# Channel mixers: where an older tile's GELU and product stand in the next tile's weight splitting

## The chip, the core and the metric

The kernel runs as one program on one core of a Trainium2 chip. The metric is the device time of one execution in microseconds (us). Three timed runs of the kernel before the change gave 1258.20, 1258.93 and 1259.92 us; the median is 1258.93 us.

Engines are named as the profile names them: PE multiplies matrices (PEld loads its stationary operand), DVE (VectorE) works element by element on whole tiles, ACT (ScalarE) applies functions and casts, POOL (GpSimd) here only issues DMAs that add into their destination, SP (SyncE) issues the plain loads.

## The reference, cut to what matters

A trunk of two layers works on 512 tokens of width 1024 in float32. Each layer ends in a convolutional GLU, the channel mixer, and the change lies in that alone:

```
def conv_glu(h, w_in, conv_w, conv_b, w_out):
    seq = h.shape[1]
    gate, val = jnp.split(h @ w_in, 2, axis=-1)
    gp = jnp.pad(gate, ((0, 0), (CONV_W - 1, 0), (0, 0)))
    conv = conv_b + sum(conv_w[j] * gp[:, j:j + seq] for j in range(CONV_W))
    return (jax.nn.gelu(conv, approximate=False) * val) @ w_out
```

`h @ w_in` has 2 x 2816 columns: 22 tiles of 128 gate columns and 128 value columns. For each tile the gate gets a causal convolution over three tokens with a bias, then GELU, and is multiplied by the value.

## The kernel before, in words

`ffn` (L435) is the channel mixer of one layer; it runs twice, once in each layer. The stage of interest is its middle: 21 of the 22 column tiles are worked off by `Seven.frame`, one call (a "frame") for each tile, and the last tile by `ending` (L648). In the trace the frames of layer 0 lie at about 390 to 587 us and those of layer 1 at about 935 to 1131 us.

**The arithmetic of a frame.** The tile's products are made by seven half-size matrix products in place of eight, so the weights first have to be added up: beside the loaded blocks G1, G2, V1, V2 of `raw` there are the sums S3, S1 (`sums`, L513, L515 in the profile), S2 (`sum2`, L520) and S4 (`sum4`, L524), all made by DVE. To keep float32 accuracy each operand is split in two parts: a rounded one, `whi`, that ACT makes with a cast (`high`, L528), and the remainder, `wlo`, which is raw minus `whi` (`lower`, L533, by DVE). One product (`prod`, L448) is 12 matmuls of 128x128 by 256 columns: 8 with `whi` (L452) and 4 with `wlo` (L454); `high_part` (L460) and `low_part` (L465) are the same in two pieces. A frame has seven of them, 84 matmuls.

**The next tile's first pair.** While frame j runs its last products, the weights of tile j+1 (`nxt`) are prepared. Its first pair is G1 beside S2: `nxt.high(G1)` casts both (128x1024) once `sum2` has made S2, and then comes the remainder, in one of two ways. For the tiles in `APART` (2, 4, ... 18) G1's remainder is made by ACT and an adding DMA (`rest1`, L505 and L506) and DVE subtracts only the S2 half (`both`, L510, 128x512). For the other tiles DVE subtracts the whole pair (`lower`, L533, 128x1024). So odd frames (3, 5, ... 17) have the short subtraction and even ones and frame 19 the long one. PE needs `whi` and `wlo` of that pair in the first product of frame j+1. Of the value pair, G2 beside V2, the remainder `wlv` is always made by ACT (`rest`, L499) and an adding DMA (L500).

**The tail of older tiles.** What is left of a tile after its products runs through the two frames behind it. In frame j the tile before, `prev`, gets `end1` (L539), `endr` (L542), `end2` (L555: the convolution's last tap and bias, by ACT), `endt` (L545: the first tap, scaled by ACT into a spare tile), `end3` (L559: the middle tap, by DVE) and `endd` (L552: an adding DMA issued by POOL that adds `endt`'s tile into the sum `c`). The tile before that one, `prev2`, gets `end4` (L562: GELU of `c`, by ACT, which has to wait for the DMA of `endd` of one frame earlier) and `end5` (L566: `c` times the value `v`, by DVE).

**What sets the order.** Nearly all of these instructions go through `keep` (L471), which holds them in the order in which the code is written, engine by engine. Each engine works its queue off in order, so an instruction that waits holds everything behind it on that engine. Small tiles (`tmp`) come from a pool of six buffers.

**The end of the stage.** `ending` is a generator that frames 19 and 20 step through. It loads the 22nd tile's gate weights (`raw_w`, L226, into a buffer that the next-to-last `wlv` leaves), casts them by ACT (L207, behind `end2` of tile 19, L555), subtracts by DVE (L215), and finishes tiles 18 to 21. The dense products of tile 21 are on L257, L258 and L261. Behind it comes `out_by_seven`, the output projection.

Of the kernel before, what the change touches and what calls it, by code (L numbers as in the profile page):

```python
# [90 lines left out]
def halved(t):  # L91
    return t.rearrange("p (a b) -> p a b", a=2)


def plain_order(ps):
    return ps.rearrange("p (b a) -> p a b", a=2)
# [37 lines left out]
def trunk_kernel(ctx, tc, A, out):  # L134
# [52 lines left out]
    def ps_f():  # L187
        return banks["F"].tile([P, S], F32, name="psf", tag="psf")
# [8 lines left out]
    def tmp(dt=F32, shape=(P, S)):  # L197
        return banks["tmp"].tile(list(shape), dt, name="tmp", tag="tmp")
# [67 lines left out]
    def run(g):  # L266
        for y in g:
            assert not callable(y) or y()
# [166 lines left out]
    def ffn(l, hp, U, T, new_x, xT, after=None, tokens=None):  # L435
# [10 lines left out]
        def prod(ps, w, x, late=False):  # L446
            (wh, wl), o, *ol = w
            ol = ol[0] if ol else o  # L448
            for ks in ((0, 1, 2), (3,)) if late else (range(4),):
                for k in ks:  # L450
                    for n in range(2):
                        PE.matmul(ps, wh[:, o + k * P:o + k * P + P], x[k][n], start=k == n == 0, stop=False)  # L452
                for k in ks:
                    PE.matmul(ps, wl[:, ol + k * P:ol + k * P + P], x[k][0], start=False, stop=k == 3)  # L454

        def high_part(ps, w, x):
            (wh, _), o = w
            for k in range(4):
                for n in range(2):
                    PE.matmul(ps, wh[:, o + k * P:o + k * P + P], x[k][n], start=k == n == 0, stop=False)  # L460

        def low_part(ps, w, x):
            (_, wl), o = w
            for k in range(4):
                PE.matmul(ps, wl[:, o + k * P:o + k * P + P], x[k][0], start=False, stop=k == 3)  # L465
# [3 lines left out]
        def keep(ins):  # L469
            return tc.keep_in_program_order(ins) if pinned[0] else ins  # L470

        h1, h2 = slice(0, 256), slice(256, 512)
        G1, S2, G2, V2, S3, S1, V1 = range(7)
        S4 = V1

        class Seven:
# [28 lines left out]
                keep(SC.activation(self.low1[:, :S], self.raw[:, G1], AF.Copy, scale=-1.0))  # L505
                GP.dma_start(self.low1[:, :S], A["ffn_in"][l, self.j, 0][:, 0:S], accum_op=ALU.add)  # L506

            def both(self):
                hi = self.high(G1)
                keep(V.tensor_tensor(self.low1[:, S:2 * S], self.raw[:, S2], hi[:, S:2 * S], op=ALU.subtract))  # L510
                self.gs = hi, self.low1

# [55 lines left out]
            def frame(self, prev2, prev, nxt, norm=None, ending=None):  # L568
                first = prev is None
                if first:  # L570
                    nxt.load()
                f1, f2, f3, self.f4 = (ps_f() for _ in range(4))
                g = self.g = tmp()
                prod(f1[:, h1], (self.gs, 0), XU(0, 0))
                if first:
                    hv = self.hv
                    turns["whi"] = (turns["whi"] + 1) % 3
                    self.h31 = self.high(S3)
                    turns["whi"] = (turns["whi"] + 1) % 3
                else:  # L580
                    hv = self.high(G2)
                keep(SC.copy(halved(g[:, h1]), plain_order(f1[:, h1])))
                if nxt and nxt.apart:
                    nxt.rest1()
                if first:
                    prod(self.f4[:, h1], ((hv, self.lows[0]), 0), XU(1, 0), True)
                if norm and not first:
                    run(norm)
                w31 = self.lower(S3, self.h31)
                if prev:  # L590
                    prev.end1()
                    prev.endr()
                prod(f2[:, h1], (self.gs, S), XT(T2), first)
                w4 = self.lower(S4, self.high(S4, S), S)
                if self.j + 2 < NFF - 1:
                    made[self.j + 2].load()
                if nxt and prev:
                    prev.end2()
                    prev.endt()
                elif prev:  # L600
                    next(ending)
                    next(ending)
                keep(V.tensor_tensor(halved(g[:, h2]), halved(g[:, h1]), plain_order(f2[:, h1]), op=ALU.subtract))
                if nxt:
                    nxt.sums()
                    nxt.sum2()
                    nxt.rest()
                if nxt and prev:
                    prev.end3()
                    prev.endd()  # L610
                if nxt and prev2:
                    prev2.end4()
                    prev2.end5()
                c = self.c = tmp()
                prod(f1[:, h2], (w31, 0), XT(T3))
                keep(V.tensor_tensor(halved(c[:, h1]), plain_order(f1[:, h2]), halved(g[:, h2]), op=ALU.subtract))
                if first:
                    next(norm)
                prod(f3[:, h2], (w31, S), XT(T1))
                if nxt:  # L620
                    if nxt.apart:
                        nxt.both()
                    else:
                        nxt.gs = nxt.lower(G1, nxt.high(G1))
                    nxt.sum4()
                else:
                    next(ending)
                if first:
                    next(norm)
                v = self.v = tmp()  # L630
                if first:
                    prod(f3[:, h1], ((hv, self.lows[1]), S, 0), XT(T4))
                else:
                    both = ((f3[:, h1], ((hv, self.low), S), XT(T4)), (self.f4[:, h1], ((hv, self.low), 0), XU(1, 0)))
                    for p in both:
                        high_part(*p)
                    low_part(*both[0])
                keep(V.tensor_tensor(v[:].rearrange("p (h a b) -> p h a b", h=2, a=2), halved(c[:, h1]).unsqueeze(1).to_broadcast([P, 2, 2, P]),
                                     f3[:].rearrange("p (h b a) -> p h a b", h=2, a=2), op=ALU.add))
                keep(V.tensor_tensor(halved(g[:, h2]), halved(g[:, h2]), plain_order(f3[:, h2]), op=ALU.subtract))  # L640
                if nxt:
                    nxt.h31 = nxt.high(S3)
                else:
                    next(ending)
                if not first:
                    low_part(*both[1])
                prod(self.f4[:, h2], (w4, 0), XU(1, 1))
# [1427 lines left out]
```

## Time and profile before

| what | us |
|---|---|
| median of the three runs | 1258.93 |
| lowest and highest run | 1258.20 and 1259.92 |
| the profiled execution's own time | 1260.42 |
| its span, first to last instruction | 1258.7 |
| PE busy (share of the span) | 1220.2 (97%) |
| DVE busy | 1028.8 (82%) |
| ACT busy | 841.8 (67%) |
| POOL busy | 150.9 (12%) |

The profiled execution took 1.7 us more than its span, and 1.5 us more than the median of the runs. PE's granted clock is at 90% or more in all 40 slices of the span, 0.997 on the mean. Busy shares are means over stages with different limits: in the frames (412 to 575 us) DVE is busy for 157.1 of 162.4 us, far above its 82%. Matmuls overlap in the records, so PE counts as busy even where its next matmul starts late; whether PE waits is read from the starts of its matmuls and from what ended the idle time, not from its share.

### The profile page before, as it was taken

The page shows a single profiled execution, that of the slowest core. Times are in us where ns is not written, and L with a number is a line of the kernel's source. Part 1 is how long each engine was busy: PE and PEld are TensorE (multiplying, and loading weights), DVE is VectorE, ACT ScalarE, POOL GpSimd, SP SyncE. Part 2 cuts the span into 40 slices and gives each one's busy share as a digit, 9 for nine tenths or more (in the row PEclk, how much of TensorE's full clock was granted, in tenths as well). Part 3 has the DMA queues.
Part 4 walks back from the last instruction along what each step waited for, and adds up shares of the span by engine and source line. Part 5 has one row for each costly group of instructions (what it writes and reads, how often), then busy time and mean ns, then how long its engine had stood idle before and what let it go on. Part 6 is the DMA issues. An engine that isn't in the chain of part 4 may idle for free.

```text
span 1258.7 us, 26447 instructions
## 1 busy us (share of the span) xinstructions
PE 1220.2 (97%) x10420; PEld 1074.6 (85%) x10420; DVE 1028.8 (82%) x1958; ACT 841.8 (67%) x1396; POOL 150.9 (12%) x180
## 2 busy tenths in 40 slices
PE   8999999999999999999999999999999999999997
PEld 6787777777788999999888878777789999998886
DVE  7976677766679999999876976658789999999785
ACT  6566668766566777776654676767767776765662
POOL 1000000000001222221220000000002322211200
PEclk9999999999999999999999999999999999999999
DMA  6355444453064989995994332234418998977961
GB/s 209 113 166 117 93 112 91 84 115 102 7 201 96 210 205 208 211 206 135 306 225 134 103 108 68 84 109 134 132 48 195 217 206 204 203 177 250 247 174 67
DMA packets 95293, 191.10 MB, mean 152 GB/s; under 512 B 22080, under 2 KB 30400, under 8 KB 95168
## 3 DMA queue, kind: packets, MB, share of 16 engines
q1 hardware_dynamic: 68592, 129.14, 32.3%
q0 software_dynamic: 26576, 60.26, 27.4%
q8 instruction: 82, 1.34, 0.4%
q14 instruction: 43, 0.35, 0.1%
HBM read 173.15 MB, written 6.29 MB: 143 GB/s over the span
## 4 chain that ended last, share of the span: by engine, by line
PE 61%; DVE 15%; ACT 9%; DMA 8%; issue 5%; POOL 1%; SPq 0%; DVEq 0%; ACTq 0%; POOLq 0%
PE psf L452 10%; PE psf L735 7%; PE psf L454 5%; PE psf L460 4%; PE psd L261 4%; PE psf L740 3%; PE psd L735 3%; PE psd L257 3%; PE psd L258 3%; DVE wlo L215 2%; DMA tmp<-r1h 2%; PE psf L465 2%; PE psd L740 2%; PE pss L1855 1%; ACT whi L207 1%
## 5 line engine op out<-in xcount | busy, mean ns | idle before, releaser
L528 ACT CAST whi<-raw 128x1024 fp32r<-128x1024 f32 (+1 forms) x168 | 150.7, 937 | 22.8 <-PE psf L452 17.4
L207 ACT CAST whi<-wraw 128x1024 fp32r<-128x1024 f32 x84 | 87.3, 1046 | 71.0 <-PE psd L258 33.8
L452 PE MATMUL psf<-th,whi 128*128 128x256 f32 x512 | 122.5, 278 | 2.0 <-ACT whi L528 2.0
L452 PE MATMUL psf<-tl,whi 128*128 128x256 f32 x512 | 122.3, 277 | 0.0
L533 DVE TENSOR_TENSOR wlo<-raw,whi 128x1024 fp32r<-128x1024 f32 (+1 forms) x108 | 109.2, 1013 | 2.0 <-ACT whi L528 1.9
L257 PE MATMUL psd<-r1h,whi 128*128 128x512 f32 x264 | 104.1, 395 | 0.0
L258 PE MATMUL psd<-r1l,whi 128*128 128x512 f32 x264 | 101.7, 386 | 0.0
L452 PEld LDWEIGHTS psf<-th,whi 128*128 128x128 f32 x512 | 98.9, 194 | 2.5 <-ACT whi L528 2.4
L452 PEld LDWEIGHTS psf<-tl,whi 128*128 128x128 f32 x512 | 99.2, 194 | 0.0
L215 DVE TENSOR_TENSOR wlo<-wraw,whi 128x1024 fp32r<-128x1024 f32 x67 | 81.8, 1221 | 20.5 <-ACT whi L207 20.5
L725 ACT CAST whi<-raw 128x1024 fp32r<-128x1024 f32 (+1 forms) x52 | 49.4, 950 | 53.1 <-PE psf L735 27.3
L726 DVE TENSOR_TENSOR wlo<-raw,whi 128x1024 fp32r<-128x1024 f32 (+1 forms) x52 | 56.7, 1101 | 30.5 <-ACT whi L725 27.8
L500 POOL DMA_DIRECT2D wlv<-in_ffn_in_dram x40 | 48.2, 1204 | 250.9 <-ACT wlv L499 193.1
L454 PE MATMUL psf<-th,wlo 128*128 128x256 f32 x504 | 77.7, 277 | 0.0
L261 PE MATMUL psd<-r1h,wlo 128*128 128x512 f32 x264 | 70.4, 389 | 0.9 <-DVE wlo L215 0.9
L555 ACT ACTIVATE tmp<-tmp,vec 128x512 f32<-128x512 f32 x44 | 35.9, 816 | 51.0 <-DVE tmp L542 51.0
L454 PEld LDWEIGHTS psf<-th,wlo 128*128 128x128 f32 x504 | 67.0, 193 | 0.1
L257 PEld LDWEIGHTS psd<-r1h,whi 128*128 128x128 f32 x264 | 49.9, 189 | 9.0 <-issue 2.1
L258 PEld LDWEIGHTS psd<-r1l,whi 128*128 128x128 f32 x264 | 50.0, 189 | 6.4 <-issue 0.7
L261 PEld LDWEIGHTS psd<-r1h,wlo 128*128 128x128 f32 x264 | 47.9, 189 | 8.0 <-DVE wlo L215 1.3
L515 DVE TENSOR_TENSOR raw<-raw 128x1024 f32<-128x1024 f32 x42 | 51.3, 1220 | 0.0
L257 PE MATMUL psd<-r2h,whi 128*128 128x512 f32 x128 | 50.3, 394 | 0.5 <-ACT r2h L1705 0.3
(622 smaller groups left out, 3739.5 us busy)
## 6 DMA issues: line engine op xcount, KB each, us to landing
raw<-in_ffn_in_dram SPq DMA_DIRECT2D x42, 512.0 KB, 5.2
raw<-in_ffn_in_dram SPq DMA_DIRECT2D x84, 256.0 KB, 5.9
wlv<-in_ffn_in_dram POOLq DMA_DIRECT2D x40, 512.0 KB, 7.8
raw<-in_ffn_out_dram SPq DMA_DIRECT2D x30, 512.0 KB, 5.8
raw<-in_ffn_out_dram POOLq DMA_DIRECT2D x24, 512.0 KB, 9.5
wraw<-in_wA_dram SPq DMA_DIRECT2D x20, 512.0 KB, 4.1
wraw<-in_w_out_dram SPq DMA_DIRECT2D x16, 512.0 KB, 4.0
wraw<-in_ffn_outp_dram SPq DMA_DIRECT2D x16, 512.0 KB, 4.7
```

The lines of the kernel that those rows point to most:

```text
L207: high = lambda: pin(SC.copy(hi[:, :n], raw))
L215: pin(V.tensor_tensor(lo[:, :n], raw, hi[:, :n], op=ALU.subtract))
L257: PE.matmul(ps, wh[:, j * P:(j + 1) * P], ah, start=start and n == 0, stop=False)
L258: dense_at[0] = PE.matmul(ps, wh[:, j * P:(j + 1) * P], al, start=False, stop=False)
L261: dense_at[0] = PE.matmul(ps, wl[:, j * P:(j + 1) * P], moving(act(k))[0], start=False, stop=stop and n == len(ks) - 1)
L452: PE.matmul(ps, wh[:, o + k * P:o + k * P + P], x[k][n], start=k == n == 0, stop=False)
L454: PE.matmul(ps, wl[:, ol + k * P:ol + k * P + P], x[k][0], start=False, stop=k == 3)
L528: keep(SC.copy(hi[:, :n], self.pair(what) if n > S else self.raw[:, what]))
L533: keep(V.tensor_tensor(lo[:, :n], self.pair(what) if n > S else self.raw[:, what], hi[:, :n], op=ALU.subtract))
L726: V.tensor_tensor(lo, s_, hi, op=ALU.subtract)
L735: PE.matmul(ps[:], a[:, k0 + i, ts], woven(hi[:, i * S:i * S + S]), start=bool(first) and (first is True or t in first) and a is act[0] an ...
L740: PE.matmul(ps[:], act[0][:, k0 + i, ts], woven(lo[:, i * S:i * S + S]), start=False, stop=bool(last) and t in last and i == n - 1)
```

## The change

In `frame`, the two calls `prev2.end4()` and `prev2.end5()` move. Before, they stood in front of `c = self.c = tmp()`, that is behind `end3` and `endd` of `prev`. Now the cast of the next tile's first pair, `nxt.high(G1)`, is taken out of `both` and of the call of `lower`; behind it stands `end4`, then the subtraction (`both` or `lower`), then `end5`, then `sum4`. Since `prev2` is there from frame 2 on and `nxt` up to frame 19, 18 frames of each layer are changed. Nothing is added or taken away.

```
@@ both @@
-            def both(self):
-                hi = self.high(G1)
+            def both(self, hi):
                 keep(V.tensor_tensor(self.low1[:, S:2 * S], self.raw[:, S2], hi[:, S:2 * S], op=ALU.subtract))
                 self.gs = hi, self.low1
@@ frame @@
                 if nxt and prev:
                     prev.end3()
                     prev.endd()
-                if nxt and prev2:
-                    prev2.end4()
-                    prev2.end5()
                 c = self.c = tmp()
                 prod(f1[:, h2], (w31, 0), XT(T3))
                 keep(V.tensor_tensor(halved(c[:, h1]), plain_order(f1[:, h2]), halved(g[:, h2]), op=ALU.subtract))
...
                 prod(f3[:, h2], (w31, S), XT(T1))
                 if nxt:
+                    hi = nxt.high(G1)
+                    if prev2:
+                        prev2.end4()
                     if nxt.apart:
-                        nxt.both()
+                        nxt.both(hi)
                     else:
-                        nxt.gs = nxt.lower(G1, nxt.high(G1))
+                        nxt.gs = nxt.lower(G1, hi)
+                    if prev2:
+                        prev2.end5()
                     nxt.sum4()
```

Lines behind `both` have a number lower by one in the changed file (L528 is L527, L562 is L561, L566 is L565), and L616, the subtraction that makes `c`, is L612.

ACT's queue in a frame, before: `rest`, the GELU, the three casts of G1, S3 and G2, the copy of `g`, and the cast of S4.

```order
L499 ACTIVATE wlv<-raw 128x1024
L562 ACTIVATE tmp<-tmp 128x512
L528 CAST whi<-raw 128x1024 x3
L582 COPY tmp<-psf 128x256
L528 CAST whi<-raw 128x512
```

The same stretch of ACT's queue now:

```order
L499 ACTIVATE wlv<-raw 128x1024
L527 CAST whi<-raw 128x1024
L561 ACTIVATE tmp<-tmp 128x512
L527 CAST whi<-raw 128x1024 x2
L581 COPY tmp<-psf 128x256
L527 CAST whi<-raw 128x512
```

The GELU has moved behind the first of the three casts.

DVE's queue in an odd frame (short subtraction), before, from `sums` to `sum4`: L559 is `end3`, L566 `end5`, L616 makes `c`, L510 is the subtraction of the next tile's first pair.

```order
L515 TENSOR_TENSOR raw<-raw 128x1024
L520 TENSOR_TENSOR raw<-raw 128x512
L559 SCALAR_TENSOR_TENSOR tmp<-tmp,vec 128x511
L566 TENSOR_TENSOR sp<-tmp 128x512
L616 TENSOR_TENSOR tmp<-psf,tmp 128x256
L510 TENSOR_TENSOR wlo<-raw,whi 128x512
L524 TENSOR_TENSOR raw<-raw 128x512
```

The same stretch of DVE's queue now:

```order
L514 TENSOR_TENSOR raw<-raw 128x1024
L519 TENSOR_TENSOR raw<-raw 128x512
L558 SCALAR_TENSOR_TENSOR tmp<-tmp,vec 128x511
L612 TENSOR_TENSOR tmp<-psf,tmp 128x256
L509 TENSOR_TENSOR wlo<-raw,whi 128x512
L565 TENSOR_TENSOR sp<-tmp 128x512
L523 TENSOR_TENSOR raw<-raw 128x512
```

`end5` has moved past `c` and the subtraction. In an even frame the same holds with the long subtraction (L533 before, L532 now, 128x1024) in L510's place. On PE, POOL and SP every instruction stands where it stood.

More of the change, by code (lines that the diff above doesn't have):

```diff
@@ L506, in rest1, with both @@
                 GP.dma_start(self.low1[:, :S], A["ffn_in"][l, self.j, 0][:, 0:S], accum_op=ALU.add)
-            def both(self):
-                hi = self.high(G1)
+            def both(self, hi):
                 keep(V.tensor_tensor(self.low1[:, S:2 * S], self.raw[:, S2], hi[:, S:2 * S], op=ALU.subtract))
@@ L610, in frame @@
                     prev.endd()
-                if nxt and prev2:
-                    prev2.end4()
-                    prev2.end5()
                 c = self.c = tmp()
@@ L620, in frame @@
                 if nxt:
+                    hi = nxt.high(G1)
+                    if prev2:
+                        prev2.end4()
                     if nxt.apart:
-                        nxt.both()
+                        nxt.both(hi)
                     else:
-                        nxt.gs = nxt.lower(G1, nxt.high(G1))
+                        nxt.gs = nxt.lower(G1, hi)
+                    if prev2:
+                        prev2.end5()
                     nxt.sum4()
```

## The prediction

> **What bounds the kernel now.** I read the page first, then the busy times of the two stretches in which the changed frames lie, from the start of `sum2` (L520) in frame 2 to its start in frame 19, 17 frames in each layer.
>
> ```profile
> 412.39:574.78 162.39, 161.79 (x1440) 161.03 (x1440) 157.10 (x238) 121.57 (x163) 43.29 (x42) 1.00 0.92 206
> 956.78:1118.53 161.75, 160.92 (x1429) 159.81 (x1428) 156.93 (x239) 121.81 (x163) 43.23 (x42) 1.00 0.92 208
> ```
>
> The columns are the length, then the busy time of PE, PEld, DVE, ACT and POOL. A frame takes 162.39/17 = 9.55 us and 161.75/17 = 9.51 us. PE and DVE are both nearly full, so I looked at how long each needs when it waits for nothing. For PE, these are the starts of the same matmul in two frames that follow each other without a wait:
>
> ```profile
> 478.82 0.28 PE L460 MATMUL psf<-th,whi 128*128 128x256 f32 x1
> ...
> 488.20 0.28 PE L460 MATMUL psf<-th,whi 128*128 128x256 f32 x1
> ```
>
> PE needs 9.38 us, or 18.76 for a pair of frames. For DVE, here is an odd frame (short subtraction) from `sum2` to `sum4`, and the even frame behind it:
>
> ```profile
> 499.11 0.69 DVE L520 TENSOR_TENSOR raw<-raw 128x512 f32<-128x512 f32 x1
> 499.71 0.75 DVE L559 SCALAR_TENSOR_TENSOR tmp<-tmp,vec 128x511 f32<-128x511 f32 x1
> 500.38 0.69 DVE L566 TENSOR_TENSOR r1l<-tmp 128x512 f32<-128x512 f32 x1
> 500.98 0.42 DVE L616 TENSOR_TENSOR tmp<-psf,tmp 128x256 f32<-128x256 f32 x1
> 501.31 0.68 DVE L510 TENSOR_TENSOR wlo<-raw,whi 128x512 fp32r<-128x512 f32 x1
> 501.91 0.69 DVE L524 TENSOR_TENSOR raw<-raw 128x512 f32<-128x512 f32 x1
> ...
> 508.09 0.69 DVE L520 TENSOR_TENSOR raw<-raw 128x512 f32<-128x512 f32 x1
> ...
> 510.63 0.69 DVE L566 TENSOR_TENSOR r1l<-tmp 128x512 f32<-128x512 f32 x1 [1.18 <-ACT tmp L562]
> ...
> 511.57 1.22 DVE L533 TENSOR_TENSOR wlo<-raw,whi 128x1024 fp32r<-128x1024 f32 x1
> 512.71 0.69 DVE L524 TENSOR_TENSOR raw<-raw 128x512 f32<-128x512 f32 x1
> ```
>
> The odd frame has no wait: 508.09 - 499.11 = 8.98 us. An even one has the long subtraction, 512.71 - 511.57 = 1.14 from start to start where the short one has 501.91 - 501.31 = 0.60, so it needs 8.98 + 0.54 = 9.52 us. A pair is 18.50 us, 0.26 under PE's. DVE has hardly any slack, then, and its waits count. Who makes it wait, in the order layer 0, layer 1:
>
> ```profile
> DVE sp L566 <- ACT tmp L562: 2.5, 4, 0.9
> DVE r1l L566 <- ACT tmp L562: 1.4, 2, 1.2
> ```
>
> ```profile
> DVE r2l L566 <- ACT tmp L562: 1.3, 2, 0.9
> DVE wlo L533 <- ACT whi L528: 1.2, 1, 1.2
> DVE sp L566 <- ACT tmp L562: 1.2, 2, 0.9
> DVE r2h L566 <- ACT tmp L562: 0.4, 1, 0.4
> ```
>
> Nearly all of it is `end5` waiting for the GELU: 3.9 us in six waits and 2.9 us in five. The GELU itself waits for the adding DMA of `endd`, and holds the cast behind it, for which then PE waits:
>
> ```profile
> 507.36 1.05 ACT L499 ACTIVATE wlv<-raw 128x1024 fp32r<-128x1024 f32 x1
> 509.97 0.63 ACT L562 ACTIVATE tmp<-tmp 128x512 f32<-128x512 f32 x1 [1.56 <-DMA tmp<-r1h]
> ```
>
> ```profile
> 511.59 0.38 PE L452 MATMUL psf<-r2h,whi 128*128 128x256 f32 x1 [0.33 <-ACT whi L528]
> ```
>
> DVE never waits for PE in these stretches; PE follows DVE and ACT.
>
> **What the change takes away.** No instruction is added or dropped. With the cast first, the GELU no longer holds it. The latest DMA above lands 509.97 - 508.09 = 1.88 us behind the start of `sum2`; the new place of the GELU is at about 1.75 in the frame (cast from 0.81, the next instruction some 0.95 behind it, below), and in an even frame `end5` comes at about 3.0, when a GELU of 0.63 that starts at 1.88 is long done. I take all eleven waits as gone, and with them PE's waits for the cast. POOL's and SP's queues stand as before, and the DMA of `endd` is issued behind `end3` as before.
>
> **What the change adds.** The subtraction needs the cast, the cast needs `sum2`. Before, DVE had `end3`, `end5` and `c` to do meanwhile; `end5` (0.60, from 500.38 to 500.98) was the cover. Now only `end3` and `c` are left. That order exists in the trace already: frame 1 has no `prev2`, so neither GELU nor `end5` stands there.
>
> ```profile
> 403.50 0.69 DVE L520 TENSOR_TENSOR raw<-raw 128x512 f32<-128x512 f32 x1
> ...
> 404.77 0.41 DVE L616 TENSOR_TENSOR tmp<-psf,tmp 128x256 f32<-128x256 f32 x1
> 405.39 0.69 DVE L510 TENSOR_TENSOR wlo<-raw,whi 128x512 fp32r<-128x512 f32 x1 [0.20 <-ACT whi L528]
> ```
>
> ```profile
> 404.31 2.00 ACT L528 CAST whi<-raw 128x1024 fp32r<-128x1024 f32 x2 [0.49 <-DVE raw L520]
> ```
>
> The first of these two casts starts 0.81 us behind the start of `sum2` (two take 2.00, one 1.05 like L499 of the same shape, so they start 0.95 apart), and DVE stands until 405.39. Without the wait L510 would have started 0.33 behind L616 (500.98 to 501.31), at 405.10; the cost is 0.29 us. I take it for every changed frame. Bounds: 0.20, the idle time alone, since an instruction that waits may lose only that; and 0.38, if `end5` in its new place waits 0.09 for the GELU in each frame (the GELU ends at about 2.38, `end5` could start at 1.89 + 0.60 = 2.49, so this needs a GELU 0.2 late). It can't be below nothing, because the chain from `sum2` over the cast to the subtraction is as long in every frame. `c` now writes a buffer that `end3`, just ahead of it, has read, and must let it end (0.75 in place of 0.66 behind its start): 0.09, hidden in the 0.29.
>
> The Trainium skill, page "VectorE: DVE Perf Modes", section "The DRAIN you can't avoid", says that the next operation does not start before the pipe is empty and that a semaphore costs nothing extra. By that a wait would cost its 0.20 alone. The trace disagrees: L510 at 501.31 started 0.33 behind an L616 that lasted 0.42.
>
> **The sum.** From `sum4` to the next `sum2` there are 508.09 - 501.91 = 6.18 us. An odd frame becomes 8.98 + 0.29 = 9.27, an even one 9.52 + 0.29 = 9.81; a pair is 19.08 and over PE's 18.76, so DVE now sets the pace. Frame 2 has the load of the GELU's table in it:
>
> ```profile
> 411.44 1.04 ACT L499 ACTIVATE wlv<-raw 128x1024 fp32r<-128x1024 f32 x1
> 412.50 1.28 ACT L562 ACT_TABLE_LOAD   x1
> 413.80 0.64 ACT L562 ACTIVATE tmp<-tmp 128x512 f32<-128x512 f32 x1
> ```
>
> Now it stands behind the cast: cast from 0.81 to about 1.86, load to 3.14, GELU to 3.80, `end5` at 3.83, `sum4` at 4.43, and the frame is 10.61. The stretch becomes 10.61 + 8 x 19.08 = 163.25 us: +0.86 in layer 0 and +1.50 in layer 1. Odd frames lose 8 x 0.29 = 2.3; even frames win, because the waits for the GELU lay there, but less. Then frame 19 up to `sum4`:
>
> ```profile
> 578.12 0.69 DVE L524 TENSOR_TENSOR raw<-raw 128x512 f32<-128x512 f32 x1
> ```
>
> ```profile
> 1122.33 0.69 DVE L524 TENSOR_TENSOR raw<-raw 128x512 f32<-128x512 f32 x1
> ```
>
> That was 578.12 - 574.78 = 3.34 without a wait, and 1122.33 - 1118.53 = 3.80 with one (the 0.4 above); now it is 3.34 + 0.29 = 3.63 in both: DVE leaves the frames 0.86 + 0.29 = 1.15 us later in layer 0, and 1.50 - 0.17 = 1.33 in layer 1. Who passes that on? The ending's first cast (L207):
>
> ```profile
> 582.23 0.81 ACT L555 ACTIVATE tmp<-tmp,vec 128x512 f32<-128x512 f32 x1 [1.42 <-DVE tmp L542]
> 583.31 1.05 ACT L207 CAST whi<-wraw 128x1024 fp32r<-128x1024 f32 x1 [0.26 <-DMA wraw<-in_ffn_in_dram]
> ```
>
> ```profile
> 1126.44 0.82 ACT L555 ACTIVATE tmp<-tmp,vec 128x512 f32<-128x512 f32 x1 [1.49 <-DVE tmp L542]
> 1127.16 1.03 ACT L207 CAST whi<-wraw 128x1024 fp32r<-128x1024 f32 x1
> ```
>
> ```profile
> 597.71 2.00 PE L261 MATMUL psd<-r2h,wlo 128*128 128x512 f32 x8 [1.17 <-DVE wlo L215]
> ```
>
> L555 waits for DVE, and L207 is right behind it: 0.72 from start to start in layer 1, 1.08 in layer 0 because of a load, so 0.36 is absorbed there. From L207 the ending runs through ACT and DVE to L261, for which PE waits, so I count the delay in full: 1.15 - 0.36 = 0.79 and 1.33, together +2.1 us. The profiled execution, 1260.42 (span 1258.7), would become 1262.5. The median of the runs is 1.5 us lower: 1258.93 + 2.1 = 1261.0. The bounds of the 0.29 move 34 frames by 0.09 each way, 3.1 us: 1257.9 to 1264.1.
>
> **Rivals.**
>
> *The cover holds (faster).* If the cast were done in time in the steady frames, DVE would need 18.50 a pair and PE set the pace: 17 x 9.38 = 159.5 us, 2.9 and 2.3 less than now, so 1253.7 at best. For it speaks that eleven waits go; against it, frame 1, where ACT had nothing else to do and the wait was there. Chance 0.07.
>
> *The waits that go were smaller to begin with (slower).* GELU lateness hangs on a DMA, and the profiled execution is 1.5 us longer than the median. If the timed runs have only half of the lateness seen here, 0.29 a frame is paid and little comes back: the 6.8 us of waits then bring 3.4 less, 1264.4 at most; PE's own pace would have hidden some of it before too, so I take 2.5: 1263.5. A late load as in the 1.2 us wait of layer 1 works the same way, since DVE has no slack left to hide it: 1262.2. It is slower by over 0.2% from 0.4 us of such a loss on. Against it: the runs differ by 1.7 us among themselves. Chance 0.22.
>
> *Only the idle time is lost.* At 0.20 a frame the 34 frames cost 3.1 us less: 1257.9. For it speaks that the profile reports 0.20 as idle, against it the starts (0.29). Chance 0.08. The Trainium skill's section on the DRAIN, named above, would have it so.
>
> *The table load empties ACT first.* In frame 2 nothing of the sort is seen: the load starts within 0.02 us of L499's end at 412.48, and the GELU 0.02 behind the load. If ACT stood for as long as the load again, 1.3 us in each layer would come on top: 1263.6. The Trainium skill, "ScalarE: Activation LUTs", section "What ACT_TABLE_LOAD costs", has a drain of about 1.38 us beside the load; the trace does not show it. Chance 0.03.
>
> **How the numbers follow.** My forecast, DVE paced by the exposed cast at about 0.29, has 0.57, at 1261.0, its own range 1260.0 to 1262.2; the other 0.03 is left for what I don't see, on either side. 0.2% is 2.5 us, about what a measurement of this kernel can tell from no change, so the border lies at 1261.45, inside that range: 0.18 of the 0.57 is beyond it. Slower: 0.18 + 0.22 + 0.03 + 0.02 = 0.45. Same: 0.39 + 0.08 = 0.47. Faster: 0.07 + 0.01 = 0.08. The range leaves out the first rival and the upper end of the bound: 1257.5 to 1263.6.
>
> **What would show it.** Right: in the profile after, the subtraction of the next tile's first pair waits about 0.2 for ACT's cast in every changed frame; `end5` waits for no GELU except in frame 2; odd frames take 9.27, even ones 9.81, hardly varying; PE waits for the S3 remainder or the like, some 0.3 a pair. Wrong: odd frames still at 8.98, or frames at PE's 9.38, or late GELUs behind the cast.

## The result and the profile after

| | before | after | ratio, 95% interval |
|---|---|---|---|
| first comparison, median | 1259.43 us (6 runs, 1257.71 to 1261.06) | 1266.64 us (6 runs, 1263.70 to 1268.56) | 1.0046 [1.0028, 1.0065] |
| the same two kernels again | 1260.76 us (35 runs) | 1264.86 us (12 runs) | 1.0032 [1.0018, 1.0046] |

The change makes the kernel slower: by 0.32% in the longer comparison (interval 0.18% to 0.46%), which is 1260.76 x 0.0032 = 4.0 us. 1261.0 was forecast, and the range up to 1263.6 does not hold 1266.64.

The profiled execution of the first comparison took 1268.56 us, its span is 1266.8. First the two stretches from `sum2` of frame 2 to `sum2` of frame 19 in that trace, the length and then PE, PEld, DVE, ACT and POOL busy:

```profile
414.66:578.68 164.02, 163.04 (x1444) 161.67 (x1444) 159.34 (x238) 120.25 (x163) 43.30 (x42) 1.00 0.90 204
963.00:1126.75 163.75, 162.79 (x1437) 160.94 (x1437) 159.33 (x238) 120.11 (x163) 43.26 (x42) 1.00 0.91 205
```

They were 162.39 and 161.75. DVE's queue in an odd frame (start of `sum2` 502.14) and in the even frame behind it (511.42); `end5` is L565 now and stands behind the subtraction:

```profile
502.14 0.69 DVE L519 TENSOR_TENSOR raw<-raw 128x512 f32<-128x512 f32 x1
502.75 0.75 DVE L558 SCALAR_TENSOR_TENSOR tmp<-tmp,vec 128x511 f32<-128x511 f32 x1
503.63 0.42 DVE L612 TENSOR_TENSOR tmp<-psf,tmp 128x256 f32<-128x256 f32 x1
504.03 0.69 DVE L509 TENSOR_TENSOR wlo<-raw,whi 128x512 fp32r<-128x512 f32 x1
504.64 0.68 DVE L565 TENSOR_TENSOR r1l<-tmp 128x512 f32<-128x512 f32 x1
505.24 0.68 DVE L523 TENSOR_TENSOR raw<-raw 128x512 f32<-128x512 f32 x1
...
511.42 0.69 DVE L519 TENSOR_TENSOR raw<-raw 128x512 f32<-128x512 f32 x1
512.03 0.74 DVE L558 SCALAR_TENSOR_TENSOR tmp<-tmp,vec 128x511 f32<-128x511 f32 x1
512.90 0.43 DVE L612 TENSOR_TENSOR tmp<-psf,tmp 128x256 f32<-128x256 f32 x1
513.35 1.22 DVE L532 TENSOR_TENSOR wlo<-raw,whi 128x1024 fp32r<-128x1024 f32 x1
514.50 0.68 DVE L565 TENSOR_TENSOR r1l<-tmp 128x512 f32<-128x512 f32 x1
```

The odd frame takes 511.42 - 502.14 = 9.28 us where it took 8.98, and the subtraction starts 504.03 - 502.14 = 1.89 us behind `sum2`, the same as in frame 1 of before (405.39 - 403.50). Without a wait it would start 0.61 + 0.67 + 0.33 = 1.61 behind it (`end3` to the next and `c` to the next as in the odd frame of before), so 0.28 us are lost. In the even frame it starts 1.93 behind `sum2`: 0.32. ACT in the same frames:

```profile
502.94 1.06 ACT L527 CAST whi<-raw 128x1024 fp32r<-128x1024 f32 x1 [0.48 <-DVE raw L519]
503.90 0.62 ACT L561 ACTIVATE tmp<-tmp 128x512 f32<-128x512 f32 x1
...
512.27 1.05 ACT L527 CAST whi<-raw 128x1024 fp32r<-128x1024 f32 x1 [0.53 <-DVE raw L519]
513.23 0.64 ACT L561 ACTIVATE tmp<-tmp 128x512 f32<-128x512 f32 x1
```

ACT stands until `sum2` lets the cast go, 0.80 behind the start of `sum2` in the odd frame, 0.85 in the even one. The subtraction starts 0.03 behind the cast's end in both (504.03 and 502.94 + 1.06 = 504.00; 513.35 and 512.27 + 1.05 = 513.32). The GELU is done 0.12 before `end5` starts in the odd frame (503.90 + 0.62 to 504.64) and 0.63 before it in the even one.

PE follows DVE, as forecast. Once in nearly every pair of frames (15 of 16 in this trace) a matmul of L454 starts about 0.39 behind the one ahead, where 0.11 is usual, and its idle time is put down to DVE's L532; one such place:

```profile
498.38 0.28 PE L452 MATMUL psf<-tl,whi 128*128 128x256 f32 x1
498.77 0.71 PE L454 MATMUL psf<-th,wlo 128*128 128x256 f32 x4
```

The idle time does not lie where the prediction put it. In front of the subtraction there is next to none (`c` ends at 504.05 and 513.33, the subtraction starts at 504.03 and 513.35); 0.13 us lie one instruction earlier, between the end of `end3` and `c` (503.50 to 503.63, 512.77 to 512.90). The part on why the prediction was wrong comes back to this. The list of waits does not show it, because it reports only longer idle times; it has to be read from the starts. What the list does show, of after in its second trace, layer 0, is that `end5` waits for the GELU once (frame 2) where it waited six times:

```profile
DVE sp L565 <- ACT tmp L561: 0.7, 1, 0.7
DVE wlo L532 <- ACT whi L527: 0.3, 1, 0.3
```

### The profile page after: what moved, and what is told of

The parts are those of the page before. It is cut to its first block, busy times and chain, and to the rows that moved or that the text cites. A ratio compares the mean times of both kernels' runs of the same rounds, so it can differ in the third digit from the quotient of the medians.

```text
span 1266.8 us, 26447 instructions
## 1 busy us (share of the span) xinstructions
PE 1225.6 (97%) x10420; PEld 1077.8 (85%) x10420; DVE 1033.5 (82%) x1958; ACT 838.0 (66%) x1396; POOL 151.0 (12%) x180
## 4 chain that ended last, share of the span: by engine, by line
PE 49%; DVE 27%; ACT 10%; issue 9%; DMA 4%; SPq 0%; DVEq 0%; ACTq 0%
PE psf L736 7%; PE psf L452 4%; PE psf L741 3%; PE psd L261 3%; PE psd L736 3%; PE psf L460 3%; PE psd L257 3%; DVE wlo L532 3%; PE psf L454 3%; DVE wlo L215 3%; PE psd L258 2%; DVE tmp L639 2%; DVE raw L514 2%; ACT whi L527 2%; PE psd L741 1%
## 5 line engine op out<-in xcount | busy, mean ns | idle before, releaser
L527 ACT CAST whi<-raw 128x1024 fp32r<-128x1024 f32 (+1 forms) x168 | 153.4, 937 | 38.9 <-DVE raw L519 23.1
L532 DVE TENSOR_TENSOR wlo<-raw,whi 128x1024 fp32r<-128x1024 f32 (+1 forms) x108 | 109.1, 1012 | 1.6 <-ACT whi L527 1.0
L257 PE MATMUL psd<-r1h,whi 128*128 128x512 f32 x264 | 104.3, 396 | 0.0
L726 ACT CAST whi<-raw 128x1024 fp32r<-128x1024 f32 (+1 forms) x52 | 49.4, 950 | 54.1 <-PE psf L736 28.1
L454 PE MATMUL psf<-th,wlo 128*128 128x256 f32 x504 | 79.8, 281 | 2.4 <-DVE wlo L532 0.8
L454 PEld LDWEIGHTS psf<-th,wlo 128*128 128x128 f32 x504 | 67.2, 194 | 5.8 <-DVE wlo L532 5.8
L257 PEld LDWEIGHTS psd<-r1h,whi 128*128 128x128 f32 x264 | 50.0, 189 | 9.2 <-issue 2.0
L257 PE MATMUL psd<-r2h,whi 128*128 128x512 f32 x128 | 50.3, 394 | 0.5 <-ACT r2h L1706 0.3
```

The source lines that it names most:

```text
L257: PE.matmul(ps, wh[:, j * P:(j + 1) * P], ah, start=start and n == 0, stop=False)
L527: keep(SC.copy(hi[:, :n], self.pair(what) if n > S else self.raw[:, what]))
L532: keep(V.tensor_tensor(lo[:, :n], self.pair(what) if n > S else self.raw[:, what], hi[:, :n], op=ALU.subtract))
```

## The experiments

All were timed in five rounds against before. "Stretch" is the 17 frames from `sum2` of frame 2 to `sum2` of frame 19, odd and even are means over eight frames each of layer 0 / layer 1, and the last column has the waits of `end5` for the GELU, total us / number, taken from the idle time just in front of each `end5` of the stretch (the list of waits, quoted in the prediction, cuts off a little differently).

| kernel | median us (runs) | ratio, 95% interval | stretch | odd | even | `end5` waits |
|---|---|---|---|---|---|---|
| before, shown ahead | | | 162.39 / 161.75 | 8.98 / 8.98 | 10.02 / 9.91 | 4.07/7, 2.44/4 |
| before_again | 1260.9 (12) | 1.0007 [0.9988, 1.0026] | 162.67 / 160.84 | 8.98 / 8.98 | 10.04 / 9.80 | 4.51/6, 2.72/6 |
| after_again | 1264.86 (12) | 1.0032 [1.0018, 1.0046] | 164.00 / 163.72 | 9.27 / 9.27 | 9.90 / 9.86 | 0.72/1, 0.72/1 |
| even_only | 1260.16 (12) | 0.9996 [0.9981, 1.0012] | 162.59 / 161.34 | 9.10 / 8.98 | 9.89 / 9.85 | 1.58/2, 0.72/1 |
| odd_only | 1262.83 (12) | 1.0020 [1.0004, 1.0035] | 163.01 / 162.59 | 9.27 / 9.27 | 9.79 / 9.74 | 2.80/5, 2.37/5 |
| product_only | 1268.02 (5) | 1.0059 [1.0047, 1.0071] | 165.37 / 165.59 | 9.27 / 9.28 | 10.01 / 10.06 | none |
| gelu_only | 1294.7 (5) | 1.0261 [1.0247, 1.0275] | 179.17 / 178.91 | 10.13 / 10.13 | 10.75 / 10.72 | 20.19/17, 19.92/17 |
| cover | 1257.26 (11) | 0.9974 [0.9962, 0.9986] | 159.08 / 159.65 | 9.11 / 9.17 | 9.52 / 9.52 | 0.47/1, 0.47/1 |
| sum4_only | 1260.45 (12) | 0.9998 [0.9987, 1.0010] | 161.62 / 161.27 | 8.98 / 8.98 | 9.90 / 9.86 | 3.56/6, 3.28/6 |

My theory, Theory A in the expectations, is that the change trades the waits of `end5` for a wait of the subtraction for the cast in every changed frame, that the second is the larger, and that what the first comparison shows beyond this is chance. The expectations give beside it what its rivals would show: Theory B, that before usually has fewer late GELUs than its first trace, and Theory C, that the loss lies outside the changed frames.

**before_again and after_again.** Both kernels once more, with no edit, to see how much of the first comparison's 7 us lies in the changed frames.

> The kernel before, unchanged, as a second sample of its trace. Measure: the stretch from the start of sum2 in frame 2 to its start in frame 19 (17 frames), 162.39 us in layer 0 and 161.75 us in layer 1 in the first trace, and the GELU waits of end5 in it (3.9 and 2.9 us). Theory A (the exposed cast on DVE is the loss, the late GELUs are as in the first trace): both stretches again 161.5 to 162.6 us, GELU waits 2.5 to 4 us each. Theory B (the late GELUs of the first trace were more than usual, so that less was to be won back): stretches of 160 to 161 us and GELU waits under 2 us. Theory C (the loss lies outside the changed frames): stretches as in A, and the rest of the span differs by some us from the first trace though nothing was changed. Ratio 1.000 in all.

> The changed kernel, as a second sample. Theory A: odd frames 9.27 us, even frames 9.86 us, stretches of 163.8 to 164.1 us in both layers as in the first trace after (164.02 and 163.75), ratio 1.003 to 1.005. Theory B: the same stretches, and a ratio above 1.004 because the kernel before is faster than its first trace. Theory C: the stretches again, but also 2 us or more at the same places outside the frames as in the first trace after (near 229 us and near 733 us); if those places are quiet this time, it was chance.

The stretches of before, and then of after:

```profile
413.02:575.69 162.67, 162.18 (x1439) 160.90 (x1438) 156.98 (x239) 121.70 (x163) 43.33 (x42) 1.00 0.91 206
958.89:1119.73 160.84, 160.35 (x1432) 159.89 (x1432) 156.95 (x238) 121.72 (x163) 43.27 (x42) 1.00 0.93 209
```

```profile
413.00:577.00 164.00, 163.14 (x1444) 161.71 (x1444) 159.32 (x239) 120.31 (x163) 43.34 (x42) 1.00 0.91 205
960.19:1123.91 163.72, 162.71 (x1436) 160.80 (x1435) 159.33 (x238) 120.06 (x163) 43.27 (x42) 1.00 0.91 205
```

This pair of traces can be read like an account. Both kernels reach frame 2 of layer 0 at the same time (413.02, 413.00), after is 577.00 - 575.69 = 1.31 late at frame 19, still 1.30 late at frame 2 of layer 1, and 1123.91 - 1119.73 = 4.18 late at its frame 19. The spans, 1259.4 and 1263.9, differ by 4.5. So all but about 0.3 us of the loss arises in the changed frames. The stretches of after come out as Theory A has them. Those of before do not quite: 162.67 is a little above the 161.5 to 162.6 that Theory A expected, and 160.84 lies where Theory B had it, though the waits in it (2.72 us) are not as few as Theory B wanted. The lateness of the GELUs differs from one execution to the next by about as much as the two theories do. The waits of `end5` that paid for part of it, in before's second trace, layer 0:

```profile
DVE r1l L566 <- ACT tmp L562: 1.9, 2, 1.4
DVE sp L566 <- ACT tmp L562: 1.9, 2, 0.9
DVE r1h L566 <- ACT tmp L562: 0.7, 1, 0.7
```

In the first comparison the spans differ by 1266.8 - 1258.7 = 8.1 us, and only 1.63 + 2.00 = 3.6 of them arise in the two stretches. After is already 414.66 - 412.39 = 2.27 late at the first changed frame, and another 2.32 come between the two layers (6.22 late at frame 2 of layer 1, 3.90 at frame 19 of layer 0). In the first of these places there is a stop of PE in an earlier stage, whose code and order are the same in both kernels. The first trace of after, and the second:

```profile
228.94 0.22 PE L1413 MATMUL pss<-Y,Tn 16*16 16x16 f32 x7 [0.26 <-ACT Y L1402]
231.17 0.33 PE L1413 MATMUL pss<-Y,Tn 16*16 16x16 f32 x25 [2.01 <-issue]
...
235.74 0.61 PE L257 MATMUL psd<-r1h,whi 128*128 128x512 f32 x1
```

```profile
230.16 0.38 PE L1413 MATMUL pss<-Y,Tn 16*16 16x16 f32 x32 [0.27 <-ACT Y L1402]
...
233.42 0.38 PE L257 MATMUL psd<-r1h,whi 128*128 128x512 f32 x1
```

From L1413 to L257 the same kernel takes 6.80 us in one trace and 3.26 in the other. PE stops for 2.0 us between two matmuls of one group while it waits for nothing that the trace shows, and then runs at a lower granted clock. One to three stretches of 3.4 us at half clock stand in every trace here, at differing places: three in after's first trace (from 232.8, 393.3 and 738.0 us on), two in its second (49.5 and 390.8), one in each trace of before (390.2; 50.0). The two that after's first trace has more stand in the two places where it falls behind outside the changed frames, and in its second trace both places are quiet, which the expectation had called chance. Half of 3.4 us, 1.7, is an estimate of what one costs where PE sets the pace. That is why the stretches of frames, not the spans, carry the comparison.

**even_only and odd_only.** The new order in every second frame, the old one in the others. `late` is true in the frames that have the new order; here for even_only, and `== 1` for odd_only:

```
+                late = self.j % 2 == 0
+                if nxt and prev2 and not late:
+                    prev2.end4()
+                    prev2.end5()
                 c = self.c = tmp()
...
                     hi = nxt.high(G1)
-                    if prev2:
+                    if prev2 and late:
                         prev2.end4()
...
-                    if prev2:
+                    if prev2 and late:
                         prev2.end5()
```

> Only even frames (long subtraction, where the late GELUs lay) have the new order; odd frames have the old one. Theory A (each frame pays its own exposed cast, DVE sets the pace): odd frames 8.98, even ones 9.86, a pair 18.84, stretch 10.66 + 8 x 18.84 = 161.4 us, 2.6 less than with the whole change and 0.4 to 1.0 less than before; ratio 0.9985 to 0.9995. Theory B: the same frames, but before has little lateness, so ratio 1.000 to 1.002. Theory C: no difference from the whole change that can be told.

> Only odd frames (short subtraction, no late GELU there) have the new order. Theory A: odd frames pay 0.29 (9.27); even frames keep the late GELU, but since the DMA has 0.29 us longer, it is late by that much less: about 9.7 in place of 10.0; pair 19.0, stretch about 163, ratio 1.001 to 1.003. If the lateness didn't depend on the frame before, the pair would be 19.3, the stretch 165 and the ratio 1.005. Theory C: no difference from the whole change that can be told.

In even_only the stretches are within 0.5 us of those of before_again: in the frames where the GELU used to be late, what is won and what is paid cancel out. The expectation had 161.4 in both layers, and layer 0 misses it by 1.2 us: its frame 15, an odd one, has a late GELU of 0.87 us that no other trace shows in an odd frame, and its frame 8 takes 10.14, as in after. In odd_only every odd frame pays 0.29 (9.27 for 8.98), 8 x 0.29 = 2.3 us a layer, and the even frames give only part of it back: 9.79 and 9.74, against 10.04 and 9.80 in before_again, so 2.0 us in layer 0 and 0.5 in layer 1. That fits the adding DMA having 0.29 us more until the GELU needs its sum; if the lateness did not depend on the frame before, the expectation had the stretch at 165. The sizes are rough, since the two traces of before differ by 0.1 a frame themselves (9.91 and 9.80 in layer 1). The two halves do not add up to the whole: -0.08 + 0.50 + 0.34 + 1.75 = 2.5 us of stretch, where after has 1.33 + 2.88 = 4.2. With the new order in both kinds of frames, the longer odd frame has no late GELU left to shorten.

**product_only and gelu_only.** One of the two moves alone. In product_only `end5` stands behind the subtraction, but the GELU stays in front of the cast. In gelu_only the GELU goes behind the cast, but `end5` stays in front of `c`:

```
@@ product_only, against after @@
+                if nxt and prev2:
+                    prev2.end4()
                 c = self.c = tmp()
...
                     hi = nxt.high(G1)
-                    if prev2:
-                        prev2.end4()
@@ gelu_only, against after @@
+                if nxt:
+                    hi = nxt.high(G1)
+                if nxt and prev2:
+                    prev2.end4()
+                    prev2.end5()
                 c = self.c = tmp()
...
-                    hi = nxt.high(G1)
-                    if prev2:
-                        prev2.end4()
...
-                    if prev2:
-                        prev2.end5()
```

> Only end5 moved behind the subtraction; the GELU stays in front of the cast. Theory A: odd frames 9.27 (the cast is exposed); in even frames the late GELU still holds the cast, now with nothing of DVE behind it to cover: 9.86 without lateness, about 10.0 with it; stretch 164.5 to 166 us, ratio 1.004 to 1.008, somewhat worse than the whole change. If the GELU's place behind the cast were what costs, this would be no slower than before.

> Only the GELU moved behind the cast; end5 stays in front of c on DVE and so waits for it. Theory A: end5 at 2.4 us behind sum2 in place of 1.3, so every frame grows by 1.15 to 1.2 us: odd 10.13, even 10.72, frame 2 about 12.1, stretch 179 us, 34 us more in all, ratio 1.026 to 1.028. If DVE didn't set the pace (PE or the transfers did), most of it would be hidden and the ratio under 1.01.

In product_only no `end5` waits, and the late GELU hits another instruction. An even frame, DVE and then ACT:

```profile
511.53 0.42 DVE L614 TENSOR_TENSOR tmp<-psf,tmp 128x256 f32<-128x256 f32 x1
512.61 1.23 DVE L532 TENSOR_TENSOR wlo<-raw,whi 128x1024 fp32r<-128x1024 f32 x1 [0.66 <-ACT whi L527]
```

```profile
511.01 0.63 ACT L561 ACTIVATE tmp<-tmp 128x512 f32<-128x512 f32 x1 [0.65 <-DMA tmp<-r1h]
511.55 2.92 ACT L527 CAST whi<-raw 128x1024 fp32r<-128x1024 f32 x3
```

The GELU waits 0.65 for the DMA, the cast stands behind it, and the subtraction waits 0.66 for the cast. The wait for the DMA has only changed its place, and the exposed cast comes on top: +0.59%. In gelu_only `end5` waits for the GELU in all 17 frames, because the GELU now starts only when the cast has ended:

```profile
DVE sp L565 <- ACT tmp L561: 9.3, 7, 2.5
DVE r1l L565 <- ACT tmp L561: 7.6, 7, 1.1
DVE r1h L565 <- ACT tmp L561: 4.4, 4, 1.1
```

(The list has frame 19 in it too.) That is 2.52 us in frame 2, where the load of the GELU's table stands in between, and about 1.1 in the others, near the length of the cast (1.05) that the GELU now stands behind. Odd frames were expected at 10.13 and even ones at 10.72, and they came out within 0.03 of that. So each move alone is worse than both together.

**cover and sum4_only.** If the loss is the lost cover, another instruction of the same length in the same place must bring it back. `sum4` is as long as `end5` (0.69) and waits for nothing here, so cover puts it in front of `c`, on top of the change. For that the updates of `v` and `g`, DVE's two instructions behind it, change places, too. sum4_only makes the same two edits to before, as the control:

```
                     prev.end3()
                     prev.endd()
+                if nxt:
+                    nxt.sum4()
                 c = self.c = tmp()
...
                         prev2.end5()
-                    nxt.sum4()
...
+                keep(V.tensor_tensor(halved(g[:, h2]), halved(g[:, h2]), plain_order(f3[:, h2]), op=ALU.subtract))
                 keep(V.tensor_tensor(v[:].rearrange("p (h a b) -> p h a b", h=2, a=2), halved(c[:, h1]).unsqueeze(1).to_broadcast([P, 2, 2, P]),
                                      f3[:].rearrange("p (h b a) -> p h a b", h=2, a=2), op=ALU.add))
-                keep(V.tensor_tensor(halved(g[:, h2]), halved(g[:, h2]), plain_order(f3[:, h2]), op=ALU.subtract))
```

> The new order, with sum4 moved in front of the subtraction that makes c, as work for DVE while ACT casts, and the two updates of v and g exchanged so that end5 isn't followed at once by v, which waits for its buffer. Theory A (the exposed cast is the whole loss, and the late GELUs stay gone): DVE back to 8.98 and 9.52 or less, 18.50 a pair, so PE's 18.76 sets the pace or a little more; frame 2 about 10.1; stretches about 160 to 160.8 us, no wait of the next tile's subtraction for the cast; 2 to 4 us less than before in all, ratio 0.9965 to 0.9985, and 6 to 8 us less than the change. If something else in the new order costs the time (the later end5, the shifted casts of S3 and G2), it stays near 1.003.

> Control: the order before, with the same move of sum4 and the same exchange of v and g, but GELU and end5 where they were. Theory A: no change, since the cast was covered and the late GELU still holds the cast and end5: odd frames 8.98, even ones 9.8 to 10.0, ratio 0.999 to 1.001. If the move of sum4 by itself brings time, it shows here.

cover is faster than before by 0.26% (1260.71 in its comparison, so 3.3 us), and with that faster than after. The stretches, and DVE's queue in an odd frame:

```profile
412.87:571.95 159.08, 159.08 (x1427) 159.08 (x1426) 156.78 (x238) 122.56 (x163) 43.26 (x42) 1.00 0.94 212
954.90:1114.54 159.64, 159.64 (x1432) 159.64 (x1431) 157.12 (x238) 122.67 (x163) 43.13 (x42) 1.00 0.92 210
```

```profile
496.96 0.69 DVE L519 TENSOR_TENSOR raw<-raw 128x512 f32<-128x512 f32 x1
497.57 0.74 DVE L558 SCALAR_TENSOR_TENSOR tmp<-tmp,vec 128x511 f32<-128x511 f32 x1
498.23 0.68 DVE L523 TENSOR_TENSOR raw<-raw 128x512 f32<-128x512 f32 x1
498.83 0.42 DVE L614 TENSOR_TENSOR tmp<-psf,tmp 128x256 f32<-128x256 f32 x1
499.17 0.68 DVE L509 TENSOR_TENSOR wlo<-raw,whi 128x512 fp32r<-128x512 f32 x1
```

Every instruction starts 0.60 to 0.66 behind a long one and 0.34 behind the short one: the cast is done in time and no wait is left here. The stretches are shorter than the 160 to 160.8 us that were expected. What sets the pace now? The starts of the same matmul of PE in three frames:

```profile
478.04 0.28 PE L460 MATMUL psf<-th,whi 128*128 128x256 f32 x1
...
487.42 0.28 PE L460 MATMUL psf<-th,whi 128*128 128x256 f32 x1
...
496.80 0.28 PE L460 MATMUL psf<-th,whi 128*128 128x256 f32 x1
```

They are 9.38 apart, PE's own need, and PE is busy for the whole of both stretches (159.08 of 159.08): PE sets the pace. sum4_only shows that the moved `sum4` by itself does nothing that can be measured. The gain belongs to the two together: the change takes the late GELUs away, and the cover takes away what the change costs.

## Why the prediction was wrong

**What was right: the path.** The subtraction starts 0.03 behind the end of the cast in the frames above and in all of frames 3 to 18 of both traces of after, so the chain from `sum2` over the cast sets when it starts, as forecast. Odd frames were to take 9.27 and take 9.27; `end5` was to wait for the GELU in frame 2 only, and does. The 0.36 that the ending absorbs in layer 0 is there as well: in the second traces, after's `sum4` of frame 19 (start 580.68) is 1.65 behind that of before (579.03), and frame 2 of layer 1 is 1.30 behind. Rival 1 had the right price for a cover that holds (159.5 a stretch; cover has 159.08 and 159.64), but the change as made takes that cover away, and the wait of `c`, below, would have kept it from that price even with a cast in time (2 x 0.21 more than 18.50 is 18.92 a pair, over PE's 18.76). One sign did not come: the subtraction itself does not sit idle for 0.2 us, because `c` in front of it has been held up by then.

**What failed: the sizes of two terms, the base and the width of the range.** The prediction gave "no difference" the highest chance (0.47) because its sum came to +2.1 us. From 1261.0 to 1266.64 there are 5.6 us.

1. *The exposed cast in even frames, 0.29.* The step "I take it for every changed frame" took the price of frame 1. There the cast starts 0.81 behind `sum2`; in even frames it starts 0.85 to 0.86 behind it, and they take 9.86 to 9.90, not 9.81. With frame 2 at 10.66 instead of 10.61 the stretch is 164.00 and 163.72 where 163.25 was forecast, and frame 19 takes 580.68 - 577.00 = 3.68 up to `sum4` in layer 0 instead of 3.63: together about 1.3 us. The trace shows what lies between. In the odd frame ACT handles one waiting instruction between the end of `sum2` and the cast, in the even frame two, and the second costs 0.055 us (the cast starts 0.11 and 0.165 behind the end of `sum2`). The additional one is for the load of G1, which landed long before (488.06 for a cast at 493.13); in odd frames `rest1` on ACT has waited for that load already. No run was made without it.
2. *The waits that are taken away.* The prediction set 162.39 and 161.75 against its stretch; the second trace of before has 162.67 and 160.84, 0.6 us less in the sum. The 1.2 us wait for a late load in layer 1 is not in it. This is the direction of rival 2, at about a quarter of its 2.5 us. With item 1 the forecast of +2.1 becomes +4.0, which is what the longer comparison measured; its interval reaches from 2.3 to 5.8 us, so that the two agree this closely is partly luck.
3. *The base.* The median of three runs was 1258.93, that of 35 runs is 1260.76: 1.8 us. What made the three faster stays open.
4. *The scatter of what was measured.* Six runs of after have 1266.64, twelve more have 1264.86: 1.8 us, which the stretches do not show (164.02 and 163.75; 164.00 and 163.72). It goes with PE's granted clock, which is on record for each run: 0.9948 on the mean of the six, 0.9967 on that of the twelve. A straight line through the twelve gives 1.0 us for each 0.001 of clock, so 0.0018 is worth 1.8 us (an estimate). The change itself does not lower the clock: the 35 runs of before have 0.9963. The range went by the bounds of one term and gave the base and the runs no width at all.

The sum is 2.0 + 1.8 + 1.8 = 5.6, the 2.0 being items 1 and 2 by the medians of the longer comparison (4.1 - 2.1). Of the chances, the border at 0.2% lay inside the forecast's own range, so 2 us in the terms decided between "no difference" and "slower".

**The wait of `c`.** The prediction counted 0.09 for `c`, which now writes a buffer that `end3` has read, and hid it in the 0.29. The rows above show 503.63 - 502.75 = 0.88 from `end3` to `c` where `end3` was followed after 0.67 before: 0.21. It is hidden as said, since the cast is later still, but barely: with a cast in time the change would have lost 0.21 of its 0.28 all the same. `sum4` in cover stands over both waits (`c` 0.60 behind it), which is why one moved instruction was enough. That `c` waits for this buffer was read from the code, and the trace agrees: of the semaphores that `c` waits for, that of `end3` is the only one that comes in the 0.25 us before `c` in 15 of the 18 even frames of after's first trace. It was not tried by itself, and `cover` takes away both waits at once. That the cast alone is enough is shown by frame 1 of before: there `c` follows `end3` without a wait, and the subtraction starts 1.89 behind `sum2` all the same.

**The two rules weighed.** By its idle time alone the wait would cost 0.20; the odd frames lost 0.29 in both traces of after. The Trainium skill, "VectorE: DVE Perf Modes", section "The DRAIN you can't avoid", has an operation start only when the pipe is empty, with nothing extra for a semaphore, and adds that an operation that is not held starts earlier. The prediction left that addition out when it said that the trace disagrees: instructions that do not wait start before the one ahead has ended (0.60 apart at 0.69 each), which fits it. What the runs add is that a wait loses this overlap too, so that it costs more than its idle time.

Frame 2, with the load of the GELU's table behind the cast, DVE and then ACT of after's second trace:

```profile
414.93 1.23 DVE L532 TENSOR_TENSOR wlo<-raw,whi 128x1024 fp32r<-128x1024 f32 x1
416.88 0.69 DVE L565 TENSOR_TENSOR sp<-tmp 128x512 f32<-128x512 f32 x1 [0.72 <-ACT tmp L561]
```

```profile
413.86 1.05 ACT L527 CAST whi<-raw 128x1024 fp32r<-128x1024 f32 x1 [0.59 <-DVE raw L519]
414.92 1.28 ACT L561 ACT_TABLE_LOAD   x1
416.21 0.63 ACT L561 ACTIVATE tmp<-tmp 128x512 f32<-128x512 f32 x1
```

The load starts 0.01 behind the cast's end and the GELU 0.01 behind the load's, and the frame takes 10.66. The drain of about 1.38 us that the Trainium skill, "ScalarE: Activation LUTs", section "What ACT_TABLE_LOAD costs", names beside the load is not there.

## What to carry to other kernels

When an instruction is moved away from a place where it waits, ask what it was covering there: here 0.60 us of product stood between a request to another engine and its answer, and its going cost about 0.3 us in each of 36 frames, more than the late GELUs it avoided. If a move is good but for the cover, put something of the same length that waits for nothing into the gap. And where the expected difference is a few us, take the base from many runs and give the range its scatter: a sum that is within 0.05 us in nearly every frame still missed by 5.6, and two thirds of that lay outside the frames.

## What the runs showed of the hardware

- PE can stop for 2.0 us between two matmuls of one group with no wait in the trace, and run at a lower clock behind it. The row of 3.4 us behind that stop in after's first trace, the granted clock being the third number from the end:

```profile
232.10:235.50 3.40, 3.40 (x32) 2.26 (x19) 1.95 (x5) 2.23 (x7) 0.00 (x0) 0.60 0.15 42
```

  The clock is 0.60 there, and 1.00 in the stretches of frames. The other trace of the same kernel has no stop there; what triggers it stays open.
- Each semaphore that an instruction of ACT waits for can cost time even when it came long ago: with one waiting instruction more in front of it the cast starts 0.055 us later (0.165 behind the end of `sum2` in place of 0.11, in the even and the odd frames of after).
- An instruction of DVE that has to wait for the one right ahead of it on its own engine (`c` behind `end3`) starts 0.13 us behind its end, while one that need not starts about 0.08 before its end. That is 0.21 us for a reused buffer, three quarters of what the wait for the other engine cost.
